# A hybrid decoder layer on one core: gate columns, weight differences, tanh and closing steps in another order

## The chip, the core and the metric

The kernel runs on one core of a Trainium2 chip. The core has five engines that take their instructions in order, each from its own queue, and wait for each other on semaphores: TensorE (PE; its weight loads are listed as PEld), VectorE (DVE), ScalarE (ACT), GpSimd (POOL) and SyncE (SP), which here issues nearly all transfers between the device memory (DRAM) and the on-chip memory. Matrix products land in eight PSUM banks of 128 x 512 fp32. The metric is the device time of one execution in microseconds; lower is better.

## The reference

One layer for 512 tokens of width 2048, batch 1, all in fp32. `z` has 7184 columns.

```python
cond = silu(c); mod = cond @ w_ada + b_ada            # 2048 x 6144
shift, scale, gate = split(mod, 3)
h = rms_norm(x, norm_g) * (1 + scale) + shift
z = h @ w_in
u_a, v_a, g_a, q_b, k_b, v_b, g_b, f_b = split(z)     # 7 x 1024 columns and 16
y_a = gelu(u_a) * (tril(W_s) @ layer_norm(gelu(v_a)) + b_s) * silu(g_a)   # 8 groups, chunks of 128 tokens
y_b = softmax(q k^T / 8 + F[t] - F[s], causal) v * silu(g_b)  # 16 heads of 64, F = cumsum(log_sigmoid(f_b + b_f))
y = concat(y_a, y_b) @ w_out                          # 2048 x 2048
out = rms_norm(x + gate * y, final_g)
```

Branch A is the spatial gating (u_a, v_a, g_a), branch B the forgetting attention (q, k, v, g, f).

## The kernel before

**Precision.** Every fp32 operand of a large product is split into a high part, rounded to the matmul type, and a low part, the difference (`split`, L65: ScalarE copies, VectorE or GpSimd subtracts). A product is three matmuls: high x high, high x low, low x high (L145 to L147 with activations streamed, L154 to L156 with weights streamed).

**Weights.** `w_tile` (L117) loads 512 KB of `w_in` into a tile tagged raw (four buffers in turn), ScalarE makes whi (L129), VectorE wlo (L130); whi and wlo have two buffers each. `col_group` (L158) computes two to four blocks of 128 columns, 16 blocks of the contraction each; after every weight tile it calls `tick()` (L133), which runs the next entry of the list `slots` (pieces of mixing or attention) and the next of `fillers` (other background work). So slots and fillers are spread over the column groups one entry per tick. A group of two blocks has four ticks, a v group four (the first one eight). Evacuations of a group follow at a raised priority. From the order of the program and its own time model the framework then sets each engine's static queue; `issue_after` pins a few instructions behind others.

**Order of stages.** The first 190 us: x, conditioning, h, and the columns u_a and the first six blocks of g_a (L325 to L408). Then:

1. `va_products` (L720): v_a into eight tiles tagged qstk, sixteen ticks. Fillers there: `spatial_weights` (L651) and the eight `sum_step(0, k)`.
2. `v_group(0)` (L681), eight ticks, with the mixing in its slots: `norm_half` (L742) normalises half of v_a and splits it into tiles tagged kstk (eight buffers; the second half's low parts on GpSimd), `mix_head` (L751) multiplies by W_s and then y by the result (L763 to L775), two heads a tick. Fillers: `sum_step(1, k)`, from here to the second g group.
3. `heads_tiles` (L415) takes over qstk and kstk for q and k. `qk_group(0)`, `g_group(0)`; `forget` (L570), a chain on 16 rows, is the first slot after v_group(0).
4. For u = 1, 2, 3: `g_group(u)` (not for u = 3), `qk_group(u)`, `v_group(u)`. The attention of the heads of u (`attention_slots`, L469: scores, log sums, probabilities into pth and ptl, values with the tile vs) takes the eight ticks after `qk_group(u)`. From u = 1 the fillers are 32 gate steps (`gate_step`, L595: 512 KB of w_ada into a raw tile, two products and sums on GpSimd), with four `gate_sum` (L640) between.
5. Columns 768 to 1023 of g_a (tiles raw_ga, ga), then `g_group(3)`, with the splitting of branch B's y (`split_b`, L816) in the slots.
6. `unit(0)` and `unit(1)` (L955), the output projection. It is computed by seven half-size products instead of eight for each half of the output columns, with sums and differences of blocks of w_out and of y (labels A11, S3, S2, S1, A12, A22, S4; four steps each, banks V, Z, X). The differences of w_out come from `sum_step`.

**`sum_step(u, k, early)`** (L614) loads four blocks of 128 x 512 of w_out, forms four differences, two on GpSimd and two on VectorE in turn (L636), and stores them to DRAM tensors `ts` (L638), from which the units load them later. For u = 0 the tiles are four of the kstk ring, for u = 1 one pth and one ptl tile, which have one buffer each.

**The gates.** `silu2` (L343) writes tanh into a tile tagged th (two buffers, shared with `tm` of the values step, L547) and then (tanh + 1) x input into a tile tagged sgB (three buffers). For blocks of g_b that exist when the values come, `values` multiplies by them (L554); blocks 6 and 7, which come later, multiply y themselves (L441).

**The tail.** In the last product (S4 of unit 1) tokens 0 to 127 are computed before tokens 128 to 255. `scale_out` (L938) takes the power -1/2 on GpSimd (L941), scales four tiles (L945 to L949) and issues four stores (L953); it is called for tokens 256 to 511 ahead of that product's last steps, and for each of the two token blocks after its own.

Of the kernel before, what the change touches and what calls it, by code (L numbers as in the profile page):

```python
# [27 lines left out]
def trunk_kernel(  # L28
# [314 lines left out]
    def silu2(dst, pt, pool, name):  # L343
        th = pool.tile([P, S], F32, name=f"th_{name}", tag="th", bufs=2)
        ta = nc.scalar.activation(th, pt, AF.Tanh, scale=0.5)
        nc.vector.scalar_tensor_tensor(dst, th, 1.0, pt, ALU.add, ALU.mult)
        return ta
# [4 lines left out]
    def evac_g(b, pt, pool):  # L352
        sg = pool.tile([P, S], F32, name=f"sgA{b}", tag="sgB", bufs=3)
        ta = silu2(sg, pt, pool, f"a{b}")
        nc.vector.scalar_tensor_tensor(y[b], sg, 0.5, y[b], ALU.mult, ALU.mult)
        return ta
# [70 lines left out]
    vs = pb.tile([P, NT, 4, P], F32R, name="vs", tag="vs")  # L427
# [7 lines left out]
    def evac_gb(b):  # L435
        def f(pt):
            sg = pb.tile([P, S], F32, name=f"sgB{b}", tag="sgB", bufs=3)
            silu2(sg, pt, pb, f"b{b}")
            sgb[b] = sg
            if b > 5:  # L440
                nc.vector.tensor_tensor(y[8 + b], y[8 + b], sg, ALU.mult)  # L441
        return f
# [26 lines left out]
    def attention_slots(u):  # L469
# [62 lines left out]
        def values(i):  # L532
# [5 lines left out]
            for buf in (pth, ptl):  # L538
                for j in range(NT):
                    nc.tensor.matmul(  # L540
                        op[:, j * P : S], vs[:, j, i, :], buf[:, OFF[j] : OFF[j] + S - j * P],
# [53 lines left out]
    def gate_step(g, i):  # L595
# [14 lines left out]
        [[dram.tile([P, 1024], F32, name=f"ts{u}_{i}_{z}") for z in range(4)] for i in range(4)]  # L610
# [3 lines left out]
    def sum_step(u, k, early):  # L614

        cs = slice(u * 1024, (u + 1) * 1024)
        js = slice((k % 2) * 512, (k % 2) * 512 + 512)
        if early:
            b11, b12, b21, b22 = [
                pb.tile([P, 512], F32, tag="kstk", name=f"ts{z}_{u}_{k}", bufs=8) for z in range(4)  # L620
            ]
            cols_ = [slice(u * 1024 + z * 512, u * 1024 + z * 512 + 512) for z in range(2)]
            nc.sync.dma_start(b11, wout_r[:, 8 + k, cols_[0]])
            nc.sync.dma_start(b12, wout_r[:, 8 + k, cols_[1]])
            nc.sync.dma_start(b22, wout_r[:, k, cols_[1]])
            nc.sync.dma_start(b21, wout_r[:, k, cols_[0]])
        else:
            a = pb.tile([P, 2, 512], F32, tag="pth", name=f"tsa{u}_{k}")
            b = pb.tile([P, 2, 512], F32, tag="ptl", name=f"tsb{u}_{k}")
            nc.sync.dma_start(a.rearrange("p s n -> p (s n)"), wout_r[:, 8 + k, cs])  # L630
            nc.sync.dma_start(b.rearrange("p s n -> p (s n)"), wout_r[:, k, cs])
            b11, b12, b21, b22 = a[:, 0], a[:, 1], b[:, 0], b[:, 1]
# [4 lines left out]
        for z, src in enumerate((b11, b12, b21, b22)):  # L637
            nc.sync.dma_start(tsum[u][k // 2][z][:, js], src)  # L638
# [42 lines left out]
    def v_group(u):  # L681
# [8 lines left out]
        with tc.high_priority(offset=EPRI):  # L690
            for t in range(NT):
                src = banks[t][:, 0:256].rearrange("p (i d) -> p i d", d=64)
                for e in range(2):
                    a, o = halves(e)
                    split(vs[:, t, e::2, a], vs[:, t, e::2, o], src[:, e::2, :])
# [82 lines left out]
    steps = [lambda u=u, k=k: sum_step(u, k, u == 0) for u in range(2) for k in range(8)]  # L778
    for i in range(8):
        fillers.extend([steps[i], lambda: None])  # L780
# [6 lines left out]
        [c_(mix_head, 4), c_(mix_head, 5)],  # L787
        [c_(mix_head, 6), c_(mix_head, 7)],
    ])
    for i in range(8, 16):  # L790
        fillers.extend([steps[i], lambda: None] + [lambda: None] * (i < 12))
    v_group(0)
    heads_tiles()
    qk_group(0)
    g_group(0)
    for u in range(1, 4):
        if u == 1:
            for g in range(4):
                for i in range(8):
                    fillers.append(lambda g=g, i=i: gate_step(g, i))  # L800
                    if g and i == 2:
# [283 lines left out]
```

## Time and profile before

| | |
|---|---|
| Runs | 924.33, 926.50, 926.22 us; median 926.22 |
| Profiled execution, its own time | 924.64 us |
| Its span (first to last instruction) | 922.9 us |
| Mean granted TensorE clock | 0.979 |
| Busy, share of the span | PE 96%, DVE 67%, ACT 48%, POOL 40% |
| Moved by DMA | 188.9 MB, mean 205 GB/s |

How to read the rows: a group row gives line, engine, operation, output tile and inputs, shape, count, then busy microseconds and the mean in ns of one, then the idle time of the engine just before and what ended it. A wait row gives who waited for whom: total us, times, longest. Busy PE time counts pipelined matmuls that overlap; the interval between two is shorter than the length of one. The granted clock is 1.00 at full speed. Between the span and the execution's own time lie 1.7 us.

### The profile page before, as it was taken

The numbers are of one execution on the slowest core, as the hardware profiler recorded it, in microseconds if no ns is written. First come the engines' busy times: TensorE is split into PE (matmuls) and PEld (weight loads), VectorE is DVE, ScalarE is ACT, GpSimd is POOL, SyncE is SP. The second block draws the span as 40 slices with busy tenths as digits, with TensorE's granted clock in tenths as the row PEclk, the third lists the DMA queues.
The fourth block names the chain that finished last, engine by engine and source line by source line (L and its number), as shares of the span: only waits on it lengthen the run. The fifth ranks groups of instructions, "written<-read, shape, count | busy, mean of one in ns | idle before, by whom it ended". The sixth has DMA issues, their size and how long they took to land.

```text
span 922.9 us, 12789 instructions
## 1 busy us (share of the span) xinstructions
PE 884.3 (96%) x4408; PEld 748.9 (81%) x4408; DVE 617.4 (67%) x1014; ACT 446.7 (48%) x775; POOL 371.7 (40%) x274
## 2 busy tenths in 40 slices
PE   6999999999999789999899999999999999999994
PEld 4888888888889667888689888898899888888883
DVE  5778888276549946545756576365664579996686
ACT  5563333542223323653636645465666657655453
POOL 1366545604335620258877888968100000000001
PEclk8999999999999889999999999999999999999998
DMA  9999995359998754236445435454333236577565
GB/s 339 354 353 356 354 311 175 112 179 381 392 343 257 240 182 119 78 115 228 138 138 172 142 123 181 152 159 140 111 107 92 69 103 214 175 256 247 189 219 194
DMA packets 132096, 188.91 MB, mean 205 GB/s; under 512 B 10544, under 2 KB 87552, under 8 KB 131520
## 3 DMA queue, kind: packets, MB, share of 16 engines
q1 hardware_dynamic: 131600, 187.53, 62.5%
q8 instruction: 35, 0.57, 0.3%
q10 hardware_dynamic: 432, 0.57, 0.2%
q14 instruction: 29, 0.24, 0.1%
HBM read 166.90 MB, written 20.97 MB: 204 GB/s over the span
## 4 chain that ended last, share of the span: by engine, by line
PE 81%; DVE 7%; DMA 6%; issue 3%; ACT 2%; POOL 0%; SPq 0%; POOLq 0%; DVEq 0%; ACTq 0%
PE s L145 6%; PE s L147 6%; PE s L146 6%; PE k L145 3%; PE k L146 3%; PE gb L145 3%; PE k L147 3%; PE gb L146 3%; PE gb L147 3%; PE vb L156 3%; PE vb L155 3%; PE vb L154 3%; PE va L155 2%; PE va L154 2%; PE va L156 2%
## 5 line engine op out<-in xcount | busy, mean ns | idle before, releaser
L604 POOL TENSOR_SCALAR gate<-gate,sc 128x512 f32<-128x512 f32 x60 | 102.5, 1718 | 37.1 <-DMA gate<-in_w_ada_dram 27.4
L130 POOL TENSOR_TENSOR wlo_st<-raw_st,whi_st 128x1024 fp32r<-128x1024 f32 (+3 forms) x36 | 68.4, 1903 | 54.1 <-ACT whi_st L129 53.2
L145 PE MATMUL s<-hh,whi_st 128*128 128x512 f32 x224 | 87.8, 395 | 1.5 <-ACT hh L267 1.5
L146 PE MATMUL s<-hl,whi_st 128*128 128x512 f32 x224 | 87.8, 392 | 0.0
L605 POOL TENSOR_TENSOR gate<-gate,gate 128x512 f32<-128x512 f32 x60 | 86.8, 1447 | 2.0
L66 ACT ACTIVATE whi_p<-p 128x1024 fp32r<-128x1024 f32 x52 | 55.1, 1060 | 54.2 <-PE woZ L906 21.5
L244 DVE SCALAR_TENSOR_TENSOR acc<-ada,sc,acc 128x512 f32<-128x512 f32 x98 | 73.9, 754 | 6.7 <-DMA ada<-in_w_ada_dram 4.0
L67 DVE TENSOR_TENSOR wlo_p<-p,whi_p 128x1024 fp32r<-128x1024 f32 x52 | 63.3, 1220 | 19.4 <-ACT whi_p L66 19.4
L147 PE MATMUL s<-hh,wlo_st 128*128 128x512 f32 x224 | 76.1, 393 | 0.0
L154 PE MATMUL vb<-whi_vb,hh 128*128 128x256 f32 (+1 forms) x256 | 72.8, 287 | 0.0
L155 PE MATMUL vb<-whi_vb,hl 128*128 128x256 f32 (+1 forms) x256 | 72.6, 287 | 0.0
L156 PE MATMUL vb<-wlo_vb,hh 128*128 128x256 f32 (+1 forms) x256 | 70.3, 285 | 0.8 <-DVE wlo_vb L130 0.8
L129 ACT ACTIVATE whi_st<-raw_st 128x1024 fp32r<-128x1024 f32 (+3 forms) x36 | 31.2, 870 | 66.6 <-PE s L146 38.9
L941 POOL TENSOR_TENSOR sfin<-sfin,nhalf 128x1 f32<-128x1 f32 x4 | 2.7, 687 | 146.4 <-DVE sfin L1037 141.9
L147 PE MATMUL q<-hh,wlo_q 128*128 128x512 f32 x128 | 50.8, 404 | 3.6 <-DVE wlo_q L130 3.6
L145 PE MATMUL k<-hh,whi_k 128*128 128x512 f32 x128 | 50.8, 397 | 3.5 <-DVE q L452 3.5
L145 PE MATMUL q<-hh,whi_q 128*128 128x512 f32 x128 | 51.8, 406 | 2.1 <-DVE mt L772 2.1
L67 DVE TENSOR_TENSOR ptl<-p,pth 128x512 fp32r<-128x512 f32 (+1 forms) x64 | 42.4, 685 | 14.2 <-ACT pth L66 11.8
L146 PE MATMUL q<-hl,whi_q 128*128 128x512 f32 x128 | 51.8, 405 | 0.0
L145 PEld LDWEIGHTS s<-hh,whi_st 128*128 128x128 f32 x224 | 42.4, 190 | 10.3 <-ACT hh L267 1.6
L487 DVE CUSTOM_DVE_ANT_0 s<-s,cmask 128x128 f32<-128x128 f32 (+1 forms) x64 | 31.1, 504 | 29.3 <-PE s L486 29.0
L146 PE MATMUL k<-hl,whi_k 128*128 128x512 f32 x128 | 50.6, 395 | 0.0
(303 smaller groups left out, 2527.2 us busy)
## 6 DMA issues: line engine op xcount, KB each, us to landing
ada<-in_w_ada_dram SPq DMA_DIRECT2D x128, 256.0 KB
gate<-in_w_ada_dram SPq DMA_DIRECT2D x32, 512.0 KB
p<-ts SPq DMA_DIRECT2D x32, 512.0 KB
p<-in_w_out_dram SPq DMA_DIRECT2D x24, 512.0 KB
raw_va<-in_w_in_dram SPq DMA_DIRECT2D x16, 512.0 KB
ts<-in_w_out_dram SPq DMA_DIRECT2D x32, 256.0 KB
ts<-ts SPq DMA_DIRECT2D x32, 256.0 KB
raw_q<-in_w_in_dram SPq DMA_DIRECT2D x16, 512.0 KB
```

What stands on the lines that cost most here:

```text
L66: a = nc.scalar.activation(hi, src, AF.Copy)
L67: return a, (eng or nc.vector).tensor_tensor(lo, src, hi.bitcast(F32), ALU.subtract)
L130: (loeng or nc.vector).tensor_tensor(lo, raw, hi.bitcast(F32), ALU.subtract)
L145: nc.tensor.matmul(pt, hi[:, j, cs], hh[k], start=(k == first), stop=False)
L146: nc.tensor.matmul(pt, hi[:, j, cs], hl[k], start=False, stop=False)
L147: nc.tensor.matmul(pt, lo[:, j, cs], hh[k], start=False, stop=(k == last))
L154: nc.tensor.matmul(o, ah[k][:, tsl], hi[:, j, :], start=(k == first), stop=False)
L155: nc.tensor.matmul(o, al[k][:, tsl], hi[:, j, :], start=False, stop=False)
L156: nc.tensor.matmul(o, ah[k][:, tsl], lo[:, j, :], start=False, stop=(k == last))
L244: nc.vector.scalar_tensor_tensor(sb if kk == KB - 1 else a, ga[:, j], col, a, ALU.mult, ALU.add)
L604: nc.gpsimd.tensor_scalar(ga[:, j], ga[:, j], sc[:, kk : kk + 1], None, ALU.mult)
L605: nc.gpsimd.tensor_tensor(a, a, ga[:, j], ALU.add)
```

## The change

The diff has these parts.

- The last two blocks of g_a are computed right after `va_products`, ahead of `v_group(0)`; the mixing's slots begin there. Heads 4 to 7 have a tick each. The tile vs is allocated after them.
- `sum_step(0, k)` has new buffers: in turn one pth and one ptl tile, or one tile tagged vs; two loads of 512 KB, two differences each on GpSimd and VectorE as before, and one store of 1 MB or two of 512 KB.
- `sum_step(1, k)` is replaced by sixteen `sum_part(1, k, p)`: half the columns each, a tile of the raw ring, two loads of 256 KB, all four differences (128 x 256) on GpSimd, one store of 512 KB. They are fillers after the gate steps.
- The gate steps are fillers from `qk_group(0)` on.
- The g groups: 0 after the first q and k columns, 2 after `v_group(1)`, 1 and 3 after the u loop. Blocks 2 and 3 of g_b now multiply y themselves.
- tanh is written into the sgB tile itself; the th tile of `silu2` is gone; sgB has four buffers in the pool pb.
- `split_b` is spread over g_group(3) one or two a tick, the last two in front of the first product.
- In `unit`, A22 comes before A12; in unit 1 x is added to u2 (`base`) between the two.
- The closing steps are written out: the first token block is summed, squared and partly stored before the second block's matmuls in program order; the multiplication by final_g is a step of its own into a new tile; the order of the last four scalings and their queues is new.

```diff
-    def silu2(dst, pt, pool, name):
-        th = pool.tile([P, S], F32, name=f"th_{name}", tag="th", bufs=2)
-        ta = nc.scalar.activation(th, pt, AF.Tanh, scale=0.5)
-        nc.vector.scalar_tensor_tensor(dst, th, 1.0, pt, ALU.add, ALU.mult)
+    def silu2(dst, pt):
+        ta = nc.scalar.activation(dst, pt, AF.Tanh, scale=0.5)
+        nc.vector.scalar_tensor_tensor(dst, dst, 1.0, pt, ALU.add, ALU.mult)
         return ta
...
-            if b > 5:
+            if y[8 + b] is not None:
                 nc.vector.tensor_tensor(y[8 + b], y[8 + b], sg, ALU.mult)
...
-    def sum_step(u, k, early):
+    def sum_step(u, k):
...
+        w = wout_r[:, :, u * 1024 : (u + 1) * 1024].rearrange("p k (s n) -> p k s n", s=2)
+        if k % 2:
+            a = [pb.tile([P, 2, 512], F32, tag=t, name=f"ts{t}{u}_{k}") for t in ("pth", "ptl")]
         else:
+            o = pb.tile([P, 4, 512], F32, tag="vs", name=f"ts{u}_{k}")
+            a = [o[:, 0:2, :], o[:, 2:4, :]]
+        nc.sync.dma_start(a[0], w[:, 8 + k])
+        nc.sync.dma_start(a[1], w[:, k])
...
+    def sum_part(u, k, p):
+
+        c = slice(p * 256, p * 256 + 256)
+        a = wp.tile([P, 4, 256], F32, tag="raw", name=f"ts{u}_{k}_{p}", bufs=4)
+        w = wout_r[:, :, u * 1024 : (u + 1) * 1024].rearrange("p k (s n) -> p k s n", s=2)
+        nc.sync.dma_start(a[:, 0:2, :], w[:, 8 + k, :, c])
+        nc.sync.dma_start(a[:, 2:4, :], w[:, k, :, c])
+        b11, b12, b21, b22 = (a[:, z, :] for z in range(4))
+        for dst, l, r in ((b11, b12, b11), (b12, b12, b22), (b22, b22, b11), (b21, b21, b22)):
+            nc.gpsimd.tensor_tensor(dst, l, r, ALU.subtract)
+        o = (k % 2) * 512 + p * 256
+        nc.sync.dma_start(tsum[u][k // 2][:, :, o : o + 256], a)
...
-    steps = [lambda u=u, k=k: sum_step(u, k, u == 0) for u in range(2) for k in range(8)]
-    for i in range(8):
-        fillers.extend([steps[i], lambda: None])
+    for k in range(8):
+        fillers.extend([lambda k=k: sum_step(0, k), lambda: None])
     va_products()
     slots.extend([
         [c_(norm_half, 0)],
         [c_(mix_head, 0), c_(mix_head, 1)],
         [c_(mix_head, 2), c_(mix_head, 3)],
         [c_(norm_half, 1)],
-        [c_(mix_head, 4), c_(mix_head, 5)],
-        [c_(mix_head, 6), c_(mix_head, 7)],
+        [c_(mix_head, 4)], [c_(mix_head, 5)], [c_(mix_head, 6)], [c_(mix_head, 7)],
     ])
-    for i in range(8, 16):
-        fillers.extend([steps[i], lambda: None] + [lambda: None] * (i < 12))
+    col_group([(G0 + 768, 256)], [(lambda pt, b=b: evac_g(b, pt, pb)) for b in range(6, 8)], "ga")
+    vs_.append(pb.tile([P, NT, 4, P], F32R, name="vs", tag="vs"))
     v_group(0)
     heads_tiles()
+    for g in range(4):
+        for i in range(8):
+            fillers.append(lambda g=g, i=i: gate_step(g, i))
+            if g and i == 2:
+                fillers.append(lambda g=g: gate_sum(g - 1))
+    parts = [lambda k=k, p=p: sum_part(1, k, p) for k in range(8) for p in range(2)]
+    fillers.extend(parts[:3] + [lambda: gate_sum(3)] + parts[3:])
     qk_group(0)
     g_group(0)
     for u in range(1, 4):
...
-        if u < 3:
-            g_group(u)
+        if u == 2:
+            g_group(2)
         qk_group(u)
         v_group(u)
...
-    col_group([(G0 + 768, 256)], [(lambda pt, b=b: evac_g(b, pt, pb)) for b in range(6, 8)], "ga")
-    slots.extend([
-        [c_(split_b, i) for i in range(4)], [c_(split_b, 4), c_(split_b, 5)], [], [],
-    ])
+    g_group(1)
+    slots.extend([[c_(split_b, i) for i in ii] for ii in ((0,), (1, 2), (3, 4), (5,))])
     g_group(3)
-    slots.extend([[c_(split_b, 6), c_(split_b, 7)]])
+    split_b(6)
+    split_b(7)
+    slots.append([])
...
+    def base(rr, g):
+
+        xr = wtile("xr3")
+        for t in range(2):
+            nc.sync.dma_start(xr[:, t, :], x[0, t * P : (t + 1) * P, g * 512 : (g + 1) * 512])
+        for t in range(2):
+            gated(rr[t], rr[t], g)
+            nc.vector.tensor_tensor(rr[t], rr[t], xr[:, t, :], ALU.add)
...
-        product(V, "A12", w_raw(0, g1, "p2"), False)
-        evac(lambda t: gated(c1[t], V[t], g1))
-        both(lambda t: piece(c1[t], t, g1))
         product(X, "A22", w_sum(2, "p4"), False)
         evac(lambda t: nc.vector.tensor_tensor(c7[t], X[t], c7[t], ALU.add))
         both(lambda t: gated(c7[t], c7[t], g1))
         both(lambda t: piece(c7[t], 2 + t, g1))
+        if u:
+            base(u2, g2)
+        product(V, "A12", w_raw(0, g1, "p2"), False)
+        evac(lambda t: gated(c1[t], V[t], g1))
+        both(lambda t: piece(c1[t], t, g1))
...
+        def norm(t, tmp):
+            s0, s1 = sfin[:, t, 0:1], sfin[:, t, 1:2]
             squares(u2[t], t, g2, tmp)
             nc.vector.scalar_tensor_tensor(s1, ssf[:, t, g2 : g2 + 1], 1.0 / D, s0, ALU.mult, ALU.add)
-            scale_out(t, g2)
+            nc.gpsimd.tensor_tensor(s1, s1, nhalf[:, 0:1], ALU.pow)
+            fin = pb.tile([P, S], F32, name=f"fin{t}", tag="sgB", bufs=4)
+            nc.vector.tensor_tensor(fin, u2[t], fgs[g2], ALU.mult)
+            r[t][g2] = fin
...
+        mm(0)
+        norm(0, total(0)[0])
+        put(0, 0, nc.scalar, nc.sync)
+        put(0, 1, nc.scalar, nc.sync)
+        mm(1)
+        tmp, last = total(1)
+        with tc.issue_after(last.ins):
+            put(0, 2, nc.vector, nc.sync)
+        with tc.issue_after(last.ins):
+            put(0, 3, nc.vector, nc.sync)
+        norm(1, tmp)
+        put(1, 3, nc.vector, nc.sync)
+        put(1, 0, nc.scalar, nc.scalar)
+        put(1, 1, nc.vector, nc.sync)
+        put(1, 2, nc.scalar, nc.scalar)
```

Here `mm(t)` is the loop of the last product's eight steps for a token block, `total(t)` multiplies Z by the gate into tmp and adds it to u2, and `put(t, g, engine, queue)` scales one tile by s1 on that engine and stores it from that queue.

More of the change, by code (lines that the diff above doesn't have):

```diff
@@ L352, in evac_g @@
     def evac_g(b, pt, pool):
-        sg = pool.tile([P, S], F32, name=f"sgA{b}", tag="sgB", bufs=3)
-        ta = silu2(sg, pt, pool, f"a{b}")
+        sg = pool.tile([P, S], F32, name=f"sgA{b}", tag="sgB", bufs=3 if pool is st else 4)
+        ta = silu2(sg, pt)
         nc.vector.scalar_tensor_tensor(y[b], sg, 0.5, y[b], ALU.mult, ALU.mult)
@@ L426, in trunk_kernel @@
     fsplit = pb.tile([16, 2, S], F32R, name="fsplit", tag="fs")
-    vs = pb.tile([P, NT, 4, P], F32R, name="vs", tag="vs")
+    vs_ = []
     wsp = pb.tile([P, 8, 2, P], F32R, name="wsp", tag="wsp")
@@ L436, in f @@
         def f(pt):
-            sg = pb.tile([P, S], F32, name=f"sgB{b}", tag="sgB", bufs=3)
-            silu2(sg, pt, pb, f"b{b}")
+            sg = pb.tile([P, S], F32, name=f"sgB{b}", tag="sgB", bufs=4)
+            silu2(sg, pt)
             sgb[b] = sg
-            if b > 5:
+            if y[8 + b] is not None:
                 nc.vector.tensor_tensor(y[8 + b], y[8 + b], sg, ALU.mult)
@@ L609, in trunk_kernel @@
     tsum = [
-        [[dram.tile([P, 1024], F32, name=f"ts{u}_{i}_{z}") for z in range(4)] for i in range(4)]
+        [dram.tile([P, 4, 1024], F32, name=f"ts{u}_{i}") for i in range(4)]
         for u in range(2)
     ]
-    def sum_step(u, k, early):
-        cs = slice(u * 1024, (u + 1) * 1024)
+    def sum_step(u, k):
         js = slice((k % 2) * 512, (k % 2) * 512 + 512)
[L618 to L626, printed above, removed]
-        else:
[L628 to L632, printed above, removed]
+        w = wout_r[:, :, u * 1024 : (u + 1) * 1024].rearrange("p k (s n) -> p k s n", s=2)
+        if k % 2:
+            a = [pb.tile([P, 2, 512], F32, tag=t, name=f"ts{t}{u}_{k}") for t in ("pth", "ptl")]
+        else:
+            o = pb.tile([P, 4, 512], F32, tag="vs", name=f"ts{u}_{k}")
+            a = [o[:, 0:2, :], o[:, 2:4, :]]
+        nc.sync.dma_start(a[0], w[:, 8 + k])
+        nc.sync.dma_start(a[1], w[:, k])
+        b11, b12, b21, b22 = (a[z // 2][:, z % 2, :] for z in range(4))
         for z, (dst, l, r) in enumerate((
@@ L694, in v_group @@
                     a, o = halves(e)
-                    split(vs[:, t, e::2, a], vs[:, t, e::2, o], src[:, e::2, :])
+                    split(vs_[0][:, t, e::2, a], vs_[0][:, t, e::2, o], src[:, e::2, :])
                 if u == 0:
@@ L796, in trunk_kernel @@
     for u in range(1, 4):
[L797 to L801, printed above, removed]
-                        fillers.append(lambda g=g: gate_sum(g - 1))
-            fillers.extend([lambda: None] * 3 + [lambda: gate_sum(3)])
-        if u < 3:
-            g_group(u)
+        if u == 2:
+            g_group(2)
         qk_group(u)
```

51 lines of the change are left out of this document (28 added, 23 removed).

## The prediction

> **What bounds the kernel now.** I read the page first: the share of each engine.
>
> ```profile
> span 922.9 us, 12789 instructions
> PE 884.3 (96%) x4408; PEld 748.9 (81%) x4408; DVE 617.4 (67%) x1014; ACT 446.7 (48%) x775; POOL 371.7 (40%) x274
> ```
>
> TensorE is busy for 884.3 of 922.9 us, and the change leaves its matmuls as they are. So only three things can move the time: idle time of TensorE, busy time at a lowered clock, and what follows the last matmul. Next the list of what TensorE waited for:
>
> ```profile
> PE mix L763 <- DVE mt L772: 3.9, 3, 2.8
> PE q L147 <- DVE wlo_q L130: 3.6, 2, 3.1
> PE k L145 <- DVE q L452: 3.5, 1, 3.5
> PE q L145 <- DVE mt L772: 2.1, 1, 2.1
> PE mix L764 <- POOL vl L67: 0.9, 1, 0.9
> PE vb L156 <- DVE wlo_vb L130: 0.8, 1, 0.8
> ```
>
> All name VectorE or GpSimd, none a weight load. Then stretches of 5 us where these waits lie (stretch, length, then busy time of PE, PEld, DVE, ACT, POOL, then granted clock, DMA share, GB/s):
>
> ```profile
> 285.00:290.00 5.00, 4.17 (x34) 3.96 (x33) 5.00 (x13) 1.56 (x3) 2.19 (x3) 1.00 0.75 228
> 310.00:315.00 5.00, 2.19 (x16) 1.78 (x14) 5.00 (x9) 2.17 (x6) 4.32 (x3) 0.90 0.51 157
> 315.00:320.00 5.00, 2.96 (x12) 2.68 (x13) 5.00 (x13) 0.93 (x5) 1.32 (x2) 0.50 0.86 261
> 320.00:325.00 5.00, 2.94 (x10) 2.46 (x10) 4.23 (x10) 0.00 (x0) 3.87 (x8) 0.50 0.57 205
> 325.00:330.00 5.00, 5.00 (x18) 3.98 (x17) 3.58 (x4) 0.00 (x0) 1.61 (x1) 0.73 0.59 223
> 335.00:340.00 5.00, 2.81 (x13) 2.00 (x11) 1.62 (x3) 0.25 (x1) 0.85 (x1) 1.00 0.56 162
> 340.00:345.00 5.00, 4.09 (x11) 3.23 (x12) 3.25 (x5) 4.94 (x6) 2.00 (x1) 0.66 0.50 128
> 345.00:350.00 5.00, 4.48 (x20) 3.38 (x19) 4.97 (x4) 1.27 (x2) 0.00 (x0) 1.00 0.43 137
> ...
> 450.00:455.00 5.00, 4.46 (x23) 3.63 (x22) 4.01 (x7) 1.69 (x5) 4.86 (x5) 1.00 0.27 76
> 455.00:460.00 5.00, 1.72 (x8) 0.98 (x6) 4.07 (x8) 4.93 (x10) 4.33 (x4) 1.00 0.62 198
> 460.00:465.00 5.00, 4.22 (x12) 3.37 (x13) 4.91 (x5) 2.53 (x7) 5.00 (x5) 0.66 0.46 140
> ```
>
> **Hole A** (285 to 350, the mixing and the first q columns): idle is 5 minus PE busy, 0.83 + 2.81 + 2.04 + 2.06 + 2.19 + 0.91 + 0.52 = 11.4 us. Busy time at clock f loses 1 - f of itself: 2.19 x 0.10 + 2.96 x 0.50 + 2.94 x 0.50 + 5.00 x 0.27 + 4.09 x 0.34 = 5.9 us. Together 17.3 us. **Hole B** (450 to 465, the second q columns): idle 0.54 + 3.28 + 0.78 = 4.6, clock 4.22 x 0.34 = 1.4, together 6.0 us. The third piece is the **tail** (start, length, engine, line):
>
> ```profile
> 909.68 0.39 PE L907 MATMUL woZ<-w3l,s 128*128 128x512 f32 x1
> ...
> 912.61 0.68 DVE L1052 TENSOR_TENSOR wide<-tmp,wide 128x512 f32<-128x512 f32 x1
> ...
> 914.97 0.75 DVE L945 SCALAR_TENSOR_TENSOR wide<-wide,sfin,fgb 128x512 f32<-128x512 f32 x1 [0.66 <-POOL sfin L941]
> ...
> 918.04 1.15 SPq L953 DMA_DIRECT2D out_dram<-c  x1
> ```
>
> The last matmul ends at 910.07, the span at 922.9: 12.8 us, with the last store issued at 918.04. Elsewhere TensorE is full, but for the first 30 us, which the change does not touch. So A, B and the tail are the whole stake: 17.3 + 6.0 of stalls and some of the 12.8.
>
> **The change, part by part.** *Half of the differences leave hole A.* What holds VectorE there is told by its own waits and, for hole B, by those of ScalarE, with the tanh of the gates beside them:
>
> ```profile
> DVE tsa L636 <- DMA tsb<-in_w_out_dram: 10.6, 2, 8.9
> ...
> ACT pth L66 <- DMA ts<-tsb: 3.4, 1, 3.4
> ...
> L345 ACT ACTIVATE th_b<-gb x4: 587/598/601, 399.1 to 471.0; 128x512 f32<-128x512 f32 x4
> ```
>
> For 8.9 us VectorE stood before a difference whose weights had not landed, and the operands that TensorE wanted (wlo_q, the forget chain of L580 to L591) were queued behind it: that is the 3.1 us wait at q and its half clock. With u=1 out of these ticks the queue cannot stop so; its SP stores, which stood ahead of raw_k, go too. I credit all of the 335 to 350 part: idle 3.62 + clock 1.39 = 5.0 us, lower bound 3 (the forget chain remains on VectorE).
>
> *The gate columns come beside the mixing.* The rest of A (12.3 us) is VectorE full while TensorE has only v columns to run. What each then has:
>
> ```profile
> 280.00:300.00 20.00, 19.17 (x151) 18.76 (x150) 19.06 (x36) 6.86 (x12) 13.83 (x19) 1.00 0.79 249
> 300.00:320.00 20.00, 15.15 (x109) 14.46 (x108) 19.98 (x39) 7.93 (x20) 11.21 (x8) 0.85 0.77 250
> ...
> 840.00:860.00 20.00, 20.00 (x90) 16.57 (x89) 10.40 (x10) 9.95 (x12) 0.00 (x0) 1.00 0.70 232
> ...
> L636 DVE TENSOR_TENSOR tsa<-tsa,tsb 128x512 f32<-128x512 f32 x2 | 2.5, 1226 | 0.0
> ...
> L130 DVE TENSOR_TENSOR wlo_ga<-raw_ga,whi_ga 128x1024 fp32r<-128x1024 f32 x4 | 4.9, 1219 | 2.5 <-ACT whi_ga L129 2.5
> ...
> L346 DVE SCALAR_TENSOR_TENSOR sgA<-th_a,sp 128x512 f32<-128x512 f32 x6 | 3.9, 682 | 0.0
> ...
> L775 DVE TENSOR_TENSOR y<-y,mt 128x512 f32<-128x512 f32 x8 | 8.0, 1030 | 0.0
> ```
>
> Two banks of 16 x 3 matmuls are 96; at 20 us for 90 that is 21.3 us of TensorE, taken from before the closing products and put here, at no net cost. TensorE's load of the stage is 19.2 + 15.2 + 21.3 = 56 us. VectorE's is 19.06 + 19.98 + 4.23 (320 to 325) = 43.3, less the difference 2.5, plus wlo_ga 4.9, plus four evacuation operations of 0.68 (2.7) = 48 us. So TensorE becomes the longer one by 8 us. But the order is serial in places: heads 4 to 7 need their halves split on GpSimd, in buffers freed by heads 0 to 3. I leave 4 us of the 12.3 standing (bounds 0, for the margin of 8; and 3.9 + 2.1 + 0.9 + 0.8 = 7.7 of waits plus their clock loss of 3.2, that is 10.9, if the mixing keeps its waits). Moved with it are its four weight loads of 512 KB on SP and the evacuation of banks 6 and 7, which the v columns' third and fourth bank now follow.
>
> The Trainium skill (TensorE: Matmul & The Clock Gate, Part 1) has the clock halved after an idle window of about 3.4 us. Here it reads 0.50 from 315 to 325 although no wait of the mixing is over 2.8 us, so I go by the rows, where short waits close together also cost clock. By the page the 4 us left would be about 3 and the sum 1 us lower.
>
> *Hole B.* The u=1 differences used the attention's pth and ptl buffers (the 3.4 us wait above). The last th_b evacuation came at 471.0, some 40 us after its columns, since th is shared with tm and sgB had three buffers; so the banks of the next k columns had to wait. In-place tanh, a fourth sgB buffer and the third g group put last take all three causes away. I credit 5.0 of 6.0 (bounds 3 and 6: the attention of u=0 now runs beside q of u=1, as u=2 beside q of u=3 does already with TensorE at 20.00 of 20, row 640:660 below).
>
> *Gate steps from the first q columns on, then sixteen small pieces.*
>
> ```profile
> L604 POOL TENSOR_SCALAR gate<-gate,sc 128x512 f32<-128x512 f32 x60 | 102.5, 1718 | 37.1 <-DMA gate<-in_w_ada_dram 27.4
> L605 POOL TENSOR_TENSOR gate<-gate,gate 128x512 f32<-128x512 f32 x60 | 86.8, 1447 | 2.0
> ...
> L819 POOL TENSOR_TENSOR y<-y 128x256 f32<-128x256 f32 x8 | 8.3, 1034 | 103.4 <-DVE y L441 89.9 <-DVE y L554 13.4
> ...
> 322.33 3.44 DMA tsb<-in_w_out_dram
> ...
> 329.51 4.51 DMA ts<-tsb
> ...
> 640.00:660.00 20.00, 20.00 (x98) 16.93 (x97) 15.14 (x27) 13.52 (x27) 6.95 (x6) 1.00 0.39 108
> ...
> 680.00:700.00 20.00, 20.00 (x161) 19.73 (x161) 10.54 (x30) 13.01 (x35) 0.00 (x0) 1.00 0.21 62
> ```
>
> A gate step is 2 x (1.72 + 1.45) = 6.3 us of GpSimd per tick, a tick without attention 24 matmuls = 5.3 us, so GpSimd falls behind by 1 us a tick in the 8 ticks of q and k, and gains it back under the attention. It did the same from 360 to 640 without a TensorE wait but hole B. A piece is 4 x 1.03 = 4.1 us; 16 are 66 us, beside 16 ticks (v, q, k, v; 590 to 705 in the timeline, 115 us), where GpSimd is nearly free. SP gets 48 issues there, and a store stands on SP until its four differences are done. VectorE loses 16 operations. I take +1 us (bounds 0 and 6, for one or two new waits of the size of hole B).
>
> *The early differences* use pth, ptl and the v tile instead of the ring that the mixing's halves need, with 3 or 4 transfers in place of 8. The stage before 280 has no TensorE wait, so nothing is gained there; the earlier start of the halves is inside the 4 us above.
>
> *Closing order.* A22 ahead of A12 lets tokens 2 and 3 finish one product (48 matmuls, 10.7 us) earlier, so their eight stores no longer stand in SP's queue. From the sum's end to the scale before are 914.97 - 913.29 = 1.7 us. With two operations of 0.68 ahead of it and nothing between, the scale starts at 0.7 + 0.7 + 1.7 = +3.1 instead of +4.9, and the last of four scales, two on each of two engines at 0.75, ends at +4.6; the last store then goes at about +5 instead of +8.0 (918.04 - 910.07). I take -3 us (bounds -1.5, the scale alone, and -5).
>
> **Sum**, against the profiled execution's own 924.64 (span 922.9 and 1.7 around it; the median of the runs is 926.22, so either may come out 1.6 off): 924.6 - 5.0 - (12.3 - 4) - 5.0 + 1 - 3 = 904.3, forecast 904.5.
>
> **Rivals.** (1) *All stalls go*: 924.6 - 17.3 - 6.0 - 4 = 897. For it the 8 us margin; against it the serial mixing. (2) *The mixing stays VectorE's*: 10.9 stay instead of 4, 911. For it 19.98 of 20 in 300 to 320. (3) *GpSimd's lag at q and k*: the zeroing of q rows (L455) and the ring of raw tiles wait behind gate steps; 8 us of lag less what the prefetch hides leaves a hole like B, 6 us: 910. Against it: from 560 to 600 q and k columns run with gate steps, and the list of TensorE's waits has none there. (4) *GpSimd's pieces hold VectorE up*: L775 takes 1.03 in the mixing, beside GpSimd, and the like-sized L346 0.68. 64 differences in 115 us are 11 in 20 us, 11.3 us at 1.03. If VectorE stood through each, 640 to 660 leaves it 4.9 and 680 to 700 leaves 9.5, so 2 to 6 us in 20 are too many; over 115 us some 23, of which I take 9 as reaching TensorE: 913. The Trainium skill (SBUF — State Buffer, Who interferes with whom) has exactly this lock, for operations with two SBUF inputs. (5) *Stalls only change place*, 924. (6) *Slower*: a piece holds a raw slot for 3.4 load + 4.1 + 4.5 store = 12 us, two slots give one piece in 6 us, a tick there lasts 7. If the store's wait on SP holds weight loads back, each piece costs TensorE a wait; from 1.4 us a piece (16 x 1.4 = 22) all is lost, and at 1.8 the time is 933. Against it: a gate step, with 6.3 us on GpSimd, did not do so.
>
> **How the numbers follow.** Forecast 0.45, (1) 0.14, (2) 0.16, (3) 0.08, (4) 0.05, (5) 0.05, (6) 0.07. The range 896 to 916 takes in the forecast with its bounds (1) to (4), 0.88, some of it beyond the ends. A change under 0.3% (2.8 us) cannot be told from none: faster 0.88, same 0.05, slower 0.07.
>
> **What would show it.** Right: between 280 and 350 TensorE near 20.00 in every 20 us and clock 1.00; no wait of VectorE for a weight of the differences after 300; the k wait of hole B gone; under 10.5 us from the last matmul to the span's end. Wrong: waits at mix of more than 4 us (rival 2), waits at q, k or scores from 330 to 400 (3), SP waiting for GpSimd and TensorE for wlo from 590 to 720 (6), or longer VectorE operations there (4).

## The result, and the profile after

| | before | after |
|---|---|---|
| Median of the runs | 926.36 us (924.33 to 930.3) | 913.21 us (910.78 to 914.39) |
| Ratio, 95% interval | | 0.985 [0.9811, 0.9888] |
| Profiled execution, its own time | 924.64 us | 910.78 us |
| Its span | 922.9 us | 909.1 us |

The change makes the kernel faster by 13.2 us. The forecast was 904.5, the range 896 to 916: the time lies in the range, but only 0.6 of the forecast gain came. The page of the changed kernel, share of each engine:

```profile
span 909.1 us, 12698 instructions
PE 880.1 (97%) x4408; PEld 744.3 (82%) x4408; DVE 603.9 (66%) x998; ACT 445.4 (49%) x775; POOL 405.9 (45%) x322
```

As many matmuls as before. Busy time is 4.2 us shorter, since less of it runs at a lowered clock. Where the rest went is told by stretches of 20 us (columns as in the prediction) where hole A and hole B were, and where TensorE now falls short:

```profile
260.00:280.00 20.00, 18.73 (x83) 15.20 (x82) 8.50 (x8) 4.08 (x5) 5.23 (x4) 1.00 0.87 299
280.00:300.00 20.00, 20.00 (x98) 16.81 (x97) 18.39 (x37) 7.05 (x10) 9.67 (x16) 1.00 0.23 56
300.00:320.00 20.00, 20.00 (x142) 18.86 (x141) 16.29 (x29) 6.45 (x11) 5.96 (x4) 1.00 0.25 58
320.00:340.00 20.00, 20.00 (x148) 19.28 (x147) 11.72 (x24) 6.53 (x18) 12.28 (x14) 1.00 0.63 187
340.00:360.00 20.00, 19.93 (x90) 15.84 (x89) 14.14 (x10) 8.61 (x10) 19.70 (x11) 1.00 0.41 129
360.00:380.00 20.00, 18.99 (x83) 15.05 (x82) 9.32 (x11) 7.46 (x11) 18.07 (x12) 1.00 0.51 160
...
400.00:420.00 20.00, 19.32 (x87) 15.47 (x86) 9.97 (x23) 12.39 (x28) 17.96 (x12) 1.00 0.48 154
420.00:440.00 20.00, 18.76 (x87) 15.07 (x87) 11.59 (x20) 9.82 (x20) 17.46 (x12) 1.00 0.60 186
440.00:460.00 20.00, 19.21 (x93) 16.14 (x92) 17.14 (x23) 11.10 (x22) 19.86 (x15) 1.00 0.48 136
...
600.00:620.00 20.00, 16.18 (x71) 13.07 (x70) 8.04 (x20) 8.34 (x18) 6.37 (x9) 0.83 0.54 160
...
680.00:700.00 20.00, 19.00 (x130) 17.55 (x130) 9.02 (x23) 11.79 (x31) 5.03 (x6) 1.00 0.68 216
```

From 280 to 360 TensorE is full, but for 0.07 us, at clock 1.00: hole A is gone. Of hole B nothing is left in its old form (the k banks). New are 1.3 us at 260 to 280, 3.7 us at 360 to 460 (1.01 + 0.68 + 1.24 + 0.79), 1.0 at 680 to 700, and at 600 to 620 3.8 us idle with 16.18 x 0.17 = 2.8 us of clock, 6.6 together. The waits of TensorE name them:

```profile
PE t L524 <- DMA q<-lt: 3.8, 1, 3.8
...
PE va L156 <- DVE wlo_va L130: 1.3, 1, 1.3
PE q L145 <- ACT whi_q L129: 1.2, 1, 1.2
PE s L484 <- ACT s L490: 1.2, 2, 1.0
...
PE o L539 <- DVE ptl L67: 0.8, 1, 0.8
PE k L145 <- ACT whi_k L129: 0.7, 1, 0.7
```

The tail, in order of time (start, length, engine, line):

```profile
899.20 0.39 PE L913 MATMUL woZ<-w3l,s 128*128 128x512 f32 x1
...
903.91 0.99 ACTq L1082 DMA_DIRECT2D out_dram<-c  x2
904.10 0.38 SPq L1082 DMA_DIRECT2D out_dram<-u  x1
```

The last matmul ends at 899.59, the span 9.5 us later instead of 12.8; the last store, ScalarE's second (x2 in the row), is issued at 904.5, 4.9 us after it, where the prediction had about 5. The books close: 922.9 - 23.3 (holes A and B) - 3.3 (tail) + 12.6 (new waits: 1.3 + 3.7 + 6.6 + 1.0) = 908.9, against a span of 909.1.

So the question for the runs is where those 12.6 us come from. What stands on SP's queue ahead of the largest of them (start, length, line):

```profile
603.62 0.53 SPq L646 DMA_DIRECT2D ts<-ts  x1
606.82 0.37 SPq L640 DMA_DIRECT2D ts<-in_w_out_dram  x1
607.29 0.42 SPq L123 DMA_DIRECT2D raw_q<-in_w_in_dram  x1
607.75 0.51 SPq L641 DMA_DIRECT2D ts<-in_w_out_dram  x1
608.30 5.17 SPq L507 DMA_DIRECT2D q<-lt  x8
```

The eight small transfers of the log sums into q (L507) have their source at 602.8, written by VectorE, and are issued from 608.30 on; the matmul that needs them starts at 612.57. Ahead of them stands a load of a piece (L640), issued 2.7 us late, when its raw slot came free. SP's waits from 560 to 720 show that this is the rule:

```profile
SPq L646 <- POOL ts L644: 26.1, 14, 5.1
SPq L123 <- DMA ts<-ts: 22.1, 10, 3.4
SPq L640 <- DMA ts<-ts: 11.5, 3, 6.9
```

A piece's store (L646) waits at the head of SP's queue for GpSimd's last subtraction, and the next load of a weight (L123) or of a piece (L640) waits for the store to land, since the tile it wants is the piece's. From 330 to 470 the same queue waits for the gate steps:

```profile
SPq L123 <- POOL gate L604: 29.6, 10, 5.5
SPq L596 <- POOL gate L604: 20.0, 5, 8.1
```

### The profile page after: what moved, and what is told of

Read it like the earlier page. It is cut to its first block, busy times and chain, and to the rows that moved or that the text cites. A ratio compares the mean times of both kernels' runs of the same rounds, so it can differ in the third digit from the quotient of the medians.

```text
span 909.1 us, 12698 instructions
## 1 busy us (share of the span) xinstructions
PE 880.1 (97%) x4408; PEld 744.3 (82%) x4408; DVE 603.9 (66%) x998; ACT 445.4 (49%) x775; POOL 405.9 (45%) x322
## 4 chain that ended last, share of the span: by engine, by line
PE 77%; DMA 10%; DVE 5%; POOL 3%; issue 2%; ACT 2%; SPq 0%; POOLq 0%; ACTq 0%; DVEq 0%
PE s L145 6%; PE s L147 6%; PE s L146 6%; PE va L156 3%; PE va L155 3%; PE va L154 3%; PE gb L145 3%; PE gb L146 3%; PE gb L147 3%; PE vb L154 3%; PE vb L156 3%; PE vb L155 3%; PE k L147 2%; PE k L146 2%; PE woZ L911 2%
## 5 line engine op out<-in xcount | busy, mean ns | idle before, releaser
L603 POOL TENSOR_SCALAR gate<-gate,sc 128x512 f32<-128x512 f32 x60 | 103.7, 1738 | 24.5 <-DMA gate<-in_w_ada_dram 11.9
L604 POOL TENSOR_TENSOR gate<-gate,gate 128x512 f32<-128x512 f32 x60 | 92.0, 1536 | 1.7
L644 POOL TENSOR_TENSOR ts<-ts 128x256 f32<-128x256 f32 x64 | 53.3, 837 | 62.8 <-DMA ts<-in_w_out_dram 43.8
L145 PE MATMUL gb<-hh,whi_gb 128*128 128x512 f32 x128 | 50.4, 393 | 0.5 <-ACT whi_gb L129 0.5
L145 PEld LDWEIGHTS s<-hh,whi_st 128*128 128x128 f32 x224 | 42.4, 190 | 10.3 <-ACT hh L267 1.6
L154 PE MATMUL va<-whi_va,hh 128*128 128x512 f32 x128 | 50.3, 393 | 0.0
```

Source lines behind the costliest of these rows:

```text
L145: nc.tensor.matmul(pt, hi[:, j, cs], hh[k], start=(k == first), stop=False)
L154: nc.tensor.matmul(o, ah[k][:, tsl], hi[:, j, :], start=(k == first), stop=False)
L603: nc.gpsimd.tensor_scalar(ga[:, j], ga[:, j], sc[:, kk : kk + 1], None, ALU.mult)
L604: nc.gpsimd.tensor_tensor(a, a, ga[:, j], ALU.add)
```

## The experiments

The change falls into four parts which together are exactly the change: the tanh in place with four sgB buffers; the order of the columns; the differences with the pieces and the earlier gate steps; the closing steps. Each was made alone on the kernel before. Then things were taken out of the changed kernel. Ratios are to the kernel before on the same chip, with 95% intervals.

| Run | Median us | Ratio |
|---|---|---|
| tanh alone | 919.07 | 0.9924 [0.9883, 0.9966] |
| columns alone | 914.09 | 0.9884 [0.9815, 0.9952] |
| differences and gate steps alone | 929.54 | 1.0039 [1.0001, 1.0078] |
| closing steps alone | 924.84 | 0.9986 [0.9946, 1.0026] |
| changed, log sums issued by ScalarE | 917.54 | 0.9895 [0.9838, 0.9953] |
| changed, without the pieces | 904.52 | 0.9770 [0.9714, 0.9827] |
| changed, without the gate steps | 913.26 | 0.9868 [0.9806, 0.9929] |
| changed, without both | 896.25 | 0.9665 [0.9623, 0.9708] |
| changed, differences and gate steps as before | 907.46 | 0.9816 [0.9769, 0.9863] |
| changed, pieces on GpSimd's queue | 930.13 | 1.0032 [0.9997, 1.0068] |
| changed, pieces and gate loads on GpSimd's queue | 958.87 | 1.0385 [1.0344, 1.0426] |
| differences as before, the second unit's on GpSimd alone | 903.83 | 0.9745 [0.9701, 0.9790] |

### The tanh alone

```diff
-        th = pool.tile([P, S], F32, name=f"th_{name}", tag="th", bufs=2)
-        ta = nc.scalar.activation(th, pt, AF.Tanh, scale=0.5)
-        nc.vector.scalar_tensor_tensor(dst, th, 1.0, pt, ALU.add, ALU.mult)
+        ta = nc.scalar.activation(dst, pt, AF.Tanh, scale=0.5)
+        nc.vector.scalar_tensor_tensor(dst, dst, 1.0, pt, ALU.add, ALU.mult)
```

> The kernel before with one part alone: tanh written into the sgB tile, sgB with four buffers. Theory (each hole has its own cause; hole B is the late evacuation of the gate banks, which waited for th and sgB): hole A stays as it is, the 3.5 us wait of the k columns on VectorE and the half clock behind it go, 5 us less: 921.4. Rival (hole B is the differences' use of pth and ptl): no change, 926, and the wait of k stays.

Measured 919.07, a gain of 7. The k wait of hole B (3.5 us for VectorE's q) is gone from the list of waits, all of hole A stays; two rows of it:

```profile
PE q L147 <- DVE wlo_q L130: 4.4, 2, 3.7
PE mix L762 <- DVE mt L771: 3.9, 3, 2.8
```

From 440 to 480 TensorE idles 0.4 us where the kernel before has 4.6. So new buffers for tanh and sgB alone are enough to remove hole B.

### The columns alone

```diff
+    col_group([(G0 + 768, 256)], [...], "ga")     # ahead of v_group(0)
...
-        if u < 3:
+        if u == 2:
             g_group(u)
...
+    g_group(1)
```

> The kernel before with one part alone: the order of the column groups (last two blocks of g_a beside the mixing, g groups 1 and 3 last, split_b as in the change). Theory: the part of hole A from 285 to 325 is the mixing without enough for TensorE, and goes: 10 to 12 us of its 12.3; the 335 to 350 part (5 us) stays, as the differences of u=1 still lie there; hole B shrinks, since only one g group stands before q of u=1: about 913. Rival (the mixing stays VectorE's with the differences beside it): half of the 12.3 stays, 920 or more, with waits at mix.

Measured 914.09, the time expected. The mixing's waits and hole B's are gone; left are

```profile
PE q L147 <- DVE wlo_q L130: 3.1, 2, 1.8
PE woV L906 <- DVE yl L67: 2.8, 2, 2.4
PE vb L156 <- DVE wlo_vb L130: 2.4, 2, 1.9
```

The q waits lie from 335 to 380, in and behind the part of hole A which the prediction gave to the differences on VectorE; the y wait of the closing products is new. The vb waits lie from 311 to 335, beside the mixing, where VectorE has the mixing and the differences of u=1 together: from 285 to 335 TensorE still loses 4.4 us (idle 1.15 + 1.88, clock 8.12 x 0.17 = 1.4). So of the 12.3 us some 8 go by the columns alone, where 10 to 12 were expected, and the rest only once the differences have left that place. Hole B goes here too: with g group 1 put last it is removed as well as with the tanh. The two gains therefore cannot be added.

### The differences and gate steps alone

> The kernel before with one part alone: differences of u=0 in new buffers, those of u=1 as sixteen pieces after the gate steps, gate steps from the first q columns on. Theory: the 335 to 350 part of hole A goes (5 us) and part of hole B, but the gate steps and the pieces bring new waits through the SP queue (in the changed kernel 4 us from 360 to 460 and 6.6 us near 600): net between 0 and -4 us, 922 to 926, with such waits to be seen in this kernel too. Rival (the new waits of the changed kernel come from the order of its columns): none of them here, -8 us or more, 918.

The edit is the diff's `sum_step`, `sum_part`, the tile vs allocated later, and the fillers' new order. Measured 929.54: slower than before by an interval that only just leaves out no change, and over 3 us worse than the theory's numbers. For the pieces the mechanism is the one it named:

```profile
PE t L525 <- DMA q<-lt: 11.7, 1, 11.7
...
PE q L145 <- DVE mt L781: 4.9, 1, 4.9
```

The log sums come 11.7 us late, and the loss from 600 to 640 (idle 4.24 + 7.50, clock 0.67 in the second stretch), together 16.0 us, is larger than what hole A and hole B give back (14.1 us). The waits at 360 to 460 which the theory expected as well are not there; more on this below. This part of the change, for which 5 us were credited, costs 3 us when it stands alone.

### The closing steps alone

> The kernel before with one part alone: A22 ahead of A12, base, and the closing steps written out. Theory: from the last matmul to the end of the span 9.5 us instead of 12.8, all else the same: 923. Rival (the tail is the store of the last tiles, whatever stands ahead of it): under 1 us, 925.5.

The edit is the diff's `unit`, `base` and closing steps. Measured 924.84, with an interval that holds both no change and the 3 us: too small to tell by times. Its trace shows the step itself, with the last matmul and the last store that SP issues (ScalarE issues one more at 924.9):

```profile
919.61 0.39 PE L907 MATMUL woZ<-w3l,s 128*128 128x512 f32 x1
...
924.51 0.40 SPq L1076 DMA_DIRECT2D out_dram<-u  x1
```

From the last matmul's end (920.0) to the span's end (929.3) it has 9.3 us where the kernel before has 12.8.

### The log sums issued by ScalarE

```diff
-                    nc.sync.dma_start(           # q<-lt, L507
+                    nc.scalar.dma_start(
```

> The changed kernel with the 64 small transfers q<-lt of the log sums issued by ScalarE instead of SP. Theory (the 3.8 us wait at the probabilities near 612 and its 6.8 us of half clock come from these transfers standing in SP's queue behind loads and stores of the differences): that wait goes, 6.6 us less than the changed kernel's 912 to 913, about 906; ScalarE pays 0.6 us for each issue, 5 us for each group of heads, beside work that leaves it half idle. Rival (the wait is the transfer's own way, or ScalarE late): the wait stays or moves to another line, 912 or more.

Measured 917.54, no faster than the changed kernel. The wait moved:

```profile
PE q L145 <- ACT whi_q L129: 4.9, 1, 4.9
```

The t wait is gone, but ScalarE stands at the last five transfers from 609.50 to 615.00 and copies whi_q right after, at 615.04. So the wait moved to another line, to a late ScalarE, as the rival had it. The load for that whi_q had itself stood in SP's queue behind a piece, whose load had waited 2.9 us for a store to land; what SP's queue alone would have cost this run does not tell.

### Without the pieces, without the gate steps, without both

```diff
-    parts = [lambda k=k, p=p: sum_part(1, k, p) for k in range(8) for p in range(2)]
+    parts = [lambda: None] * 16
...
-            fillers.append(lambda g=g, i=i: gate_step(g, i))
+            fillers.append((lambda g=g: nc.gpsimd.memset(gate[:, g, :], 0.0)) if i == 0 else (lambda: None))
```

Without the pieces unit 1 uses the differences of unit 0; without the gate steps the gate is the bias alone. TensorE's work stays as it is.

> The changed kernel without the sixteen pieces: the differences for the second half of the output columns are not computed, and the second unit reads those of the first. Theory: the waits at 612 (6.6 us with clock) and 682 (1.0 us) go, the small ones from 360 to 460 (3.7 us) stay: about 905. Rival (the new waits come from the order of the columns): they stay, 912.

> The changed kernel without the gate steps: the adaLN gate is only its bias, the 32 loads of w_ada and their sums on GpSimd are left out, the pieces stay in the same ticks. Theory: the waits from 360 to 460 (3.7 us, weights late on SP behind loads that wait for GpSimd) go, the one at 612 stays: about 909. Rival (they come from the attention beside q of u=1): they stay, 912.

> The changed kernel without the pieces and without the gate steps (both left out as in the two runs before). Theory: only the 1.3 us wait at 267 and the tail remain beyond the first 30 us: about 901. It bounds what any better placement of this work can reach. Rival (the order of the columns has waits of its own): 905 or more, with waits at lines that are not fed by SP.

Without both: 896.25, and after the first 30 us TensorE's list of waits is empty. That is as low as any placement of the two could bring this order of the products. Gate steps alone put 8.3 us on it (904.52), pieces alone 17.0 (913.26), both together also 17.0 (913.21). Without the pieces the wait at 612 and the one after 680 are gone, and those from 360 to 460 are left, one of them longer; without the gate steps TensorE waits for nothing from 330 to 470, and the log sums wait twice as long. One row of each, in this order:

```profile
PE q L145 <- ACT whi_q L129: 2.8, 1, 2.8
```

```profile
PE t L524 <- DMA q<-lt: 7.8, 1, 7.8
```

So each of the two has waits that go with it, and the theories' numbers for the pieces (905) and for both (901, bettered by 5) came near.

For the pieces the run with the differences and gate steps alone agrees: the log sums were late there too, in the old order of the columns. For the gate steps it shows something else. There they start at 304.0, 69 us ahead of the first scores (373.2), and SP's weight loads wait 60.3 us in 16 waits for them from 330 to 480, more than in the changed kernel. Yet from 340 to 480 TensorE idles only 0.6 us. The gate steps' 3.7 us thus need something that the changed kernel has beside them: the new order of the columns, or the mixing without its stall (from 300 to 340 that run still loses TensorE 9 us, in which GpSimd and the loads can catch up). No run tells the two apart.

That dropping the gate steps alone gains nothing was not expected: SP's waits for the pieces' subtractions grew from 26.1 to 43.7 us in that run. Why the pieces then fall worse stays open.

### The differences and gate steps put back

> The changed kernel with the differences and the gate steps put back where the kernel before had them; what is left of the change is the in-place tanh, the column order and the closing steps. Theory (of the changed kernel's stalls the one at 600 to 620 us, 6.6 us, and the one after 680, 1.0 us, come from the sixteen pieces, and some 4 us at 360 to 460 from the gate steps): these go, and what comes back are the waits that the columns alone showed at 300 to 380 and 740 to 760, of which the in-place tanh takes at most the part that hangs on q's free buffer; by the single parts 926 - 7 - 12 - 1.5 = 905.5 if nothing overlaps, and about 911 because the columns and the tanh both take away the 6 us at 450 to 465. So 905 to 911 us, below the changed kernel. Rival (the later differences are what keeps 300 to 380 free, and they pay for themselves): 914 to 918 us.

Measured 907.46. The theory's range held. By the two medians this is 5.8 us below the changed kernel, but the intervals of the two ratios overlap. The trace is clearer: from 380 to 780 TensorE is busy 400.00 of 400 us at clock 1.00, and what is left of the holes is this:

```profile
PE q L147 <- DVE wlo_q L130: 2.8, 2, 2.2
PE vb L156 <- DVE wlo_vb L130: 2.1, 2, 1.5
```

The gate steps, which start at 394.4 here and at 328.9 in the changed kernel, cost TensorE nothing, with nearly the same work on GpSimd (105.2 + 85.5 us, there 103.7 + 92.0). What differs is what stands beside them: here the scores of the attention, from 392.7 on; there the steps run ahead of it for 58 us (scores from 387.4 on).

### The pieces, and then the gate loads, on GpSimd's own queue

```diff
     def sum_part(u, k, p):
-        nc.sync.dma_start(a[:, 0:2, :], w[:, 8 + k, :, c])     # and the other load and the store
+        nc.gpsimd.dma_start(a[:, 0:2, :], w[:, 8 + k, :, c])
...
     def gate_step(g, i):
-        nc.sync.dma_start(ga, ada_r[:, 2 * i : 2 * i + 2, 2, g * 512 : (g + 1) * 512])
+        nc.gpsimd.dma_start(ga, ada_r[:, 2 * i : 2 * i + 2, 2, g * 512 : (g + 1) * 512])
```

> The changed kernel with the loads and the store of the sixteen pieces issued on GpSimd's own queue instead of SyncE's; nothing else is changed. Theory (SyncE's queue is in order and stands behind a piece's store, which waits for GpSimd's last subtraction: 26.1 us in 14 such waits): SyncE no longer waits for POOL's subtractions, the 3.8 us wait for q's next load at 608 to 612 us goes, 908 to 910 us. Rival (the weight loads wait for the buffer that a piece holds, 22.1 us in 10 waits, whichever queue issues its store): those waits stay, the wait at 600 to 620 us stays in another place, 912 to 915 us; a third of GpSimd's time for the issues would make it over 915 us.

> As the run with the pieces on GpSimd's queue, and the 32 loads of the gate steps issued there too. Theory: SyncE's 20.0 us of waits in 5 gate loads at 330 to 470 us go as well, and with them the 4 us of small TensorE waits at 360 to 460 us; 904 to 907 us. Rival (the loads of weights wait for the buffers that the gate steps hold, 29.6 us in 10 waits, and GpSimd's steps come no earlier): no more than 1 us below the run with the pieces alone on GpSimd's queue.

Both fell the other way: 930.13 and 958.87. In the first SP no longer waits for the subtractions, but for one wait of 0.3 us, as the theory had it; its weight loads, however, wait three times as long for the slots (560 to 740):

```profile
SPq L123 <- DMA ts<-ts: 74.7, 9, 13.6
```

A slot is held longer because GpSimd itself is now slower with a piece (duration least, median, most, then first and last start; and GpSimd's waits):

```profile
L640 POOL DMA_DIRECT2D ts<-in_w_out_dram x16: 727/735/930, 563.5 to 698.9; - x16
L641 POOL DMA_DIRECT2D ts<-in_w_out_dram x16: 722/730/742, 564.4 to 699.7; - x16
L646 POOL DMA_DIRECT2D ts<-ts x16: 718/738/747, 579.4 to 709.4; - x16
```

```profile
POOL ts L646 <- issue: 17.0, 7, 5.3
...
POOL ts L641 <- issue: 10.5, 5, 2.8
```

48 issues at 0.73 us are 35 us of GpSimd, where SP took 0.41, 0.50 and 0.57 in the median on these three lines, and 27.5 us more pass idle before them: together 62.5 of the 180 us, the third for which that run's rival named over 915. The weight loads do wait for the buffer, as the rival had it, whichever queue issues the store. But the same edit made each piece slower, so it does not show what the buffer alone costs. In the second run the weight loads wait 59.6 us in 10 for the gate steps as well (330 to 480), where the changed kernel has 29.6 in 10. That GpSimd must generate such a transfer's descriptors itself is what the Trainium skill says (Perfetto Trace Analysis, DMA Instruction — SWDGE (GPSIMD)); the 0.73 us rows agree.

### The second unit's differences on GpSimd alone

```diff
-            (nc.vector if z % 2 else nc.gpsimd).tensor_tensor(dst, l, r, ALU.subtract)
+            (nc.vector if early and z % 2 else nc.gpsimd).tensor_tensor(dst, l, r, ALU.subtract)
```

This stands on the run with the differences and gate steps put back, where VectorE still waited 6.0 us for one difference's transfer.

> The run with the differences and the gate steps put back, with one edit: GpSimd takes all four subtractions of each of the second unit's eight steps, where VectorE took two. In that run VectorE stands 6.0 us in one wait for a difference's transfer and 2.7 us in two for loads, and TensorE then 2.8 us for wlo_q of VectorE and 2.1 us for wlo_vb, all at 300 to 380 us; 1.8 us more are the half clock. Theory (the in-order VectorE is what turns a late transfer into a wait of the products): both waits go or halve, with the clock some 4 to 6 us, 902 to 904 us. Rival (it is the weight loads, held back in SyncE's queue behind the stores of the differences, 23 us there in 14 waits at 280 to 380): GpSimd's steps take twice as long, the stores come later, and the products wait as long for whi_q or wlo_q, 906 to 910 us, with waits of ScalarE's halves instead of VectorE's.

Measured 903.83, inside the theory's 902 to 904. Both waits of that run's trace are gone, and one other has come, from the list of TensorE's waits:

```profile
PE mix L763 <- POOL vl L67: 3.1, 1, 3.1
```

GpSimd, which takes all of these subtractions, is late with one low part for the mixing. With the clock behind it, 0.77 and 0.55 in two stretches of 5 us, that wait costs 5.8 us in this trace, nearly as much as the two that went. The execution that was profiled took 910.75, 7 us over the median, and most of that lies where the kernels do not differ. Its granted clock from 20 to 40 us was 0.50, in the run with the differences put back 0.91:

```profile
20.00:40.00 20.00, 18.58 (x90) 18.40 (x89) 7.65 (x14) 8.86 (x18) 2.22 (x2) 0.50 1.09 352
```

So its trace need not show what the executions near the median do at the mixing. By the medians the edit gains 3.6 us on the run it stands on, with intervals that overlap. This version beats both kernels: its ratio of 0.9745 [0.9701, 0.9790] lies clear of the changed kernel's 0.985 [0.9811, 0.9888], by 9.4 us between the medians.

## Why the prediction was right, and where it was not

*Differences out of hole A, -5.0*: this stall is gone in the trace, and VectorE has no wait for a difference's weights after 300. The credit was right for the place. But the step is only one side of the part that carries it, and the last run takes these waits away by handing GpSimd all the subtractions where they stood, for one new wait at the mixing.

*Gate columns beside the mixing, -8.3 with 4 us left standing*: all 12.3 went, nothing is left standing; the serial places did not show. It took two parts, though: with the columns alone 4.4 us stayed, of VectorE's low parts for v beside the differences. The 8 us by which TensorE's load was to outweigh VectorE's, which took those differences as gone, was then enough. Rival 2 is out. Its price was also too low: 10.9 us leaves out the 1.35 us of clock at 325 to 330, so a mixing that kept its waits would have kept all of the 12.3.

*Hole B, -5.0 of 6.0*: all 6.0 went. Of the three causes named, the tanh and sgB alone, or the order of the columns with its g group put last alone, remove it; they were not three shares of one sum.

*Early differences, at nothing*: 1.3 us in the trace, the va wait for wlo_va at 260 to 280. No trace without this part has that wait; of those with it, this one, the differences alone (1.2) and the gate loads on GpSimd's queue (1.8) have it, the other five do not. So it comes and goes, and pricing it at nothing was near enough.

*Tail, -3*: 3.3.

*Gate steps and sixteen pieces, +1 with bounds 0 and 6*: this is the term that failed. By the trace it is 3.7 + 6.6 + 1.0 = 11.3 us, nearly twice the upper bound; by the run without both, 17.0 us (its span lies 14.5 lower). Two steps of the argument for it were wrong. First, for the pieces the prediction looked at GpSimd, "nearly free" from 590 on; GpSimd had the time, and 64 subtractions at 837 ns (53 us) are even less than the 66 reckoned. What a piece takes is a raw slot, and places in SP's queue. Rival 6 describes that mechanism, and it got only 0.07, because "a gate step, with 6.3 us on GpSimd, did not do so". But a gate step has no store: nothing of it stands on SP waiting for GpSimd's result, and its slot is free when GpSimd has read it. A piece's slot is free when its store has landed. Second, the gate steps were priced at nothing in their new place because from 360 to 640 they had cost nothing. They had run beside the attention there, from 387 on; in the changed kernel the first eight or so run in bare ticks of q and k, where the prediction's own reckoning has GpSimd behind by 1 us a tick. Rival 3 gave that lag 6 us; it is 3.7 in the trace. Bare ticks alone are not enough for it: with the differences and gate steps alone the first steps stood in such ticks too, and TensorE lost next to nothing there.

So rivals 3 and 6 were both true in part: the mechanism of rival 6, at two places instead of sixteen, and so at 7.6 us (6.6 + 1.0) instead of 22 or more. What TensorE waited for at those places was not a weight's low part, the sign that was named, but the log sums and ScalarE's scores, which stood behind the pieces or behind weights that came late through them. Rival 5, that stalls only change place, holds for nearly half: of the 26.6 us taken away 12.6 came back elsewhere. The forecast's errors of the other sign, 4 us in hole A, 1 in hole B, 0.3 in the tail, hide nearly half of it: 904.3 - 4.0 - 1.0 - 0.3 + 10.3 + 1.3 = 910.6, against 910.78 measured for the profiled execution. Without those errors it would have been 915.9, at the very end of the range; that the time lies well inside it is luck.

Rival 4 (GpSimd's pieces hold VectorE up) has its sign in the trace, but small and off the path. From 560 to 720 the same operations of VectorE are longer with the pieces than in the run without them, first with, then without:

```profile
L130 DVE TENSOR_TENSOR wlo_k<-raw_k,whi_k 128x1024 fp32r<-128x1024 f32 x6 | 8.8, 1470 | 10.1 <-ACT whi_k L129 10.1
L130 DVE TENSOR_TENSOR wlo_k<-raw_k,whi_k 128x1024 fp32r<-128x1024 f32 x6 | 7.4, 1226 | 9.8 <-ACT whi_k L129 9.7
```

Over all its operations of like shape that is 5.0 us, where the rival reckoned with some 23, and TensorE waits there only for the log sums (3.8) and for ScalarE's scores (1.0).

## What to carry to other kernels

When background work gets a place in a ring of buffers that a critical stream also uses, price it by how long it holds the slot, until its store has landed, and by what stands behind its wait on the in-order queue that issues both; the free time of the engine that does its arithmetic says little. Moving the issue to another engine is no way out if that engine is slow at issuing and its work is what holds the slot: here it cost 17 us and 46 us. And build the parts of a bundle alone: of these four two gained, one was too small to tell and one lost a little, and the bundle with the losing one put back and one `if` changed in its place beats the whole.

## What the hardware showed that was not expected

A transfer issued by GpSimd took 0.73 us of that engine in the median (0.72 to 0.93), with up to 5.3 us idle before it, against 0.41 to 0.57 us in the medians on SP for transfers of the same tiles.

The clock fell after short waits too. In the changed kernel the 3.8 us wait was followed by a granted clock of 0.60 and 0.72 in two stretches of 5 us (2.8 us lost). In the run with the differences put back a wait of 2.2 us, with another of 0.6 shortly before it, was enough for 0.66 over 5 us:

```profile
340.00:345.00 5.00, 3.46 (x8) 2.77 (x9) 4.03 (x9) 1.97 (x6) 2.19 (x1) 0.66 0.78 240
```

The waits of up to 1.2 us at 360 to 460 of the changed kernel cost no clock at all. The Trainium skill (TensorE: Matmul & The Clock Gate, Part 1) names an idle window of about 3.4 us; the first case agrees with it, the second does not, as hole A did not.

The clock of the first 40 us came out in two ways with the same instructions. In the profiled executions of the closing steps alone (931.02, where the median is 924.84) and of the last run (910.75, median 903.83) it was 0.50 all through 20 to 40 us, although TensorE was busy for 18.58 of these 20 us; in the twelve other traces it was 0.83 or 0.91. At 0.50 against 0.83 to 0.91 these 18.58 us lose 6 to 8 us more, about as much as the two executions lie above their medians (6.2 and 6.9).
